# A decoder trunk whose instruction order comes from a planner: six of the planner's numbers and two orders changed

## Chip, cores, metric

One core of a Trainium2 chip runs the whole program. The metric is device time of one execution in microseconds (us). TensorE is called PE, VectorE DVE, ScalarE ACT, GpSimd POOL and SyncE, which issues the DMAs, SP, as in the profile.

## What is computed

Two layers over a sequence of 512 rows of 1024 numbers, all in float32. Of the reference, cut:

```python
for l in range(2):
    h = x @ w_in[l]                      # one projection for all branches
    a  = diff_attention(...)             # 4 heads, two maps each: p0 - lam * p1
    bo = dsa_attention(...)              # 4 query heads, one key/value head; an indexer of
                                         # 8 heads picks the 128 best keys of each query
    co = forgetting_attention(...)       # 4 heads, logits + cumulative log forget gate
    mixed = concat(a, bo, co) * silu(gate)
    x = layer_norm(alpha * x + mixed @ w_out[l])
```

## The kernel before

**Precision.** A float32 operand is split into a high part in fp32r and the rest (`split`: ACT casts the high part, then DVE or POOL subtracts it). A product takes three matmuls: high by high, low by high, high by low. Tiles ending in `h`/`hi` and `l`/`lo` are these parts (`xh`, `xl`, `whi`, `wlo`). All matmuls stand in `mm` (L375), all transpositions of 128 x 128 blocks in `transpose` (L378), all ACT work at L345, DVE work at L353, POOL work at L365, DMAs at L370.

**Units.** Attention goes by units of two heads or maps: `d` (differential), `f` (forgetting) and `s` (sparse), in the order of the table `UNITS` (L26). A unit runs over four blocks of 128 query rows (i = 0 to 3). For each block PE computes the scores of 128(i+1) keys into a PSUM bank `w`; DVE adds the mask and takes the minimum (`negm`, the form CUSTOM_DVE in the profile, ISA in an order); ACT takes the exponent (`p`); for `d` units DVE combines two maps, for `f` and `s` units ACT scales; PE transposes `p`; ACT and DVE split the result into `pt`; PE multiplies it with the values. There are eight PSUM banks for all of this and for the projections, so a matmul that opens a bank waits until the last reader of what stood there is done.

**Indexer and top-k.** `index_scores` (L887) fills the score tiles `acc` of blocks 1 to 3 from the four groups `iq`, of two indexer heads each, whose order stands in `HEAD` (L31). `topk` (L910) then takes, in 16 rounds per block, the 8 largest (MAX8) and strikes them out (MATCH_REPLACE8): 96 steps on DVE per layer, after which three TENSOR_SCALAR make masks of `acc`. The `s` units wait for these masks.

**Projections.** Between the units PE does the input projections of the layer, one block of 128 or 256 columns at a time. The weights of a block come as two halves (`raw`, 256 KB each, a ring of 4), and each half is split into `whi` and `wlo` (`Weights.prep`, L504). Query and key blocks go through the rotation: ACT copies the bank to `tg`, four DMAs swap the halves (`tg<-tg`), DVE and POOL multiply and add, ACT casts (`qk<-tg`), DVE or POOL subtract the rest, and for keys four DMAs copy between partition halves (`qk<-qk`).

**The order.** The kernel doesn't leave the order to a scheduler. `Flow` (L109) is a planner that runs while the program is built: `run` picks the first task, by priority, whose condition holds at the planned time of PE, and every instruction gets a planned start from a cost and from the latencies between engines. `emit` writes the instructions in the order of these starts. On the chip each engine then works through its own list in that order and waits on semaphores, whatever the plan thought of the time. SP's list is one queue too: a DMA that waits for its source holds up those behind it.

The numbers that the change touches are used in these places:

```python
flow.issue("pe", width(o) / 2.262 + 2, ...)                      # mm, L374
return min(self.gap(key, self.now, cond[2])[1] - SLACK, cond[3]) # ready_at, L267
yield "idle", "dve", cost + 100, start + TOPK_SPAN * n / 96      # topk, L919
... max(w.ready.values()) <= flow.now + READY for w in blocks)   # can_go, L1184
ready = split(hi[:, c], lo[:, c], raw, 0 if self.early else PREP_BIAS)  # prep, L515
```

The first is the planned time of a matmul on PE in ns. By the second and third a top-k step goes out when the plan sees a gap on DVE within `SLACK` ns, and at the latest at its share of `TOPK_SPAN`. By the fourth a projection may be chosen when its weights will be split within `READY` ns. In the last, `PREP_BIAS` is how many ns later than DVE the plan lets POOL end a subtraction for weights and still gives it to POOL; it counts while a top-k is under way.

Of the kernel before, what the change touches and what calls it, by code (L numbers as in the profile page):

```python
# [22 lines left out]
NEG = -1e30  # L23
TAKEN = -3e38
TOPK = min(256, S // 4)
UNITS = [("d", 0), ("f", 1), ("f", 0), ("d", 1), ("d", 3), ("d", 2), ("s", 1), ("s", 0)]  # L26
CONSTS = 3 * 512 + 128 + 9

LATE = 6
EARLY = 3  # L30
HEAD = [("kk", 0), ("dk", 0), ("dq", 0), ("dv", 0), ("iq", 1), ("iq", 0), ("iq", 3), ("iq", 2)]  # L31
INDEX_AT = 1
EXTRA = [("gate", 4)]
PROMPT = 5
# [4 lines left out]
BANKS = {"w": 8}  # L39
SHARE = {"proj": "w", "s": "w", "t": "w"}  # L40
RINGS = {"qk": 14, "tg": 7, "p": 4, "pt": 6, "vv": 4, "a": 2, "whi": 4, "wlo": 4}
SLACK = 1000
READY = 500
WAITING = 1
TOPK_SPAN = 112500
MARGIN = 0
BIAS = 2000
COLD = 5500
SPARE = 2
LNBIAS = 2000  # L50
LAST = 96
PREP_BIAS = 3500
RAW = 4

DQ, DK, DV = 0, 512, 1024
# [6 lines left out]
def early(l):  # L62
    return HEAD[:EARLY] + ([] if l else EXTRA)


def plan(l):
# [28 lines left out]

    for nm, j in early(l) + HEAD[EARLY:]:
        add(nm, j)
    for f, j in UNITS:
        for nm in {"d": ("dq", "dk", "dv"), "s": ("sq",), "f": ("fq", "fk", "fv")}[f]:
# [9 lines left out]
class Flow:  # L109
# [148 lines left out]
    def ready_at(self, cond):  # L258
# [7 lines left out]
        if kind == "idle":  # L266
            return min(self.gap(key, self.now, cond[2])[1] - SLACK, cond[3])  # L267
        times = sorted(self.banks[SHARE.get(key, key)] if kind == "bank" else self.free[key])
# [29 lines left out]
def tile_hybrid_decoder(  # L298
# [26 lines left out]
    flow = Flow()  # L325


    def width(ap):
        n = 1
        for d in ap.shape[1:]:  # L330
            n *= d
        return n
# [34 lines left out]
    def dma(o, i):  # L367
        inside = [v for v in (o, i) if not v.tensor.name.startswith(("in_", "out_"))]
        outs, ins = [v for v in inside if v is o], [v for v in inside if v is i]
        return flow.issue("sp", 640 if ins else 475, outs, ins, lambda: nc.sync.dma_start(o, i),  # L370
                          width(o) * o.shape[0] * 4)

    def mm(o, lhsT, rhs, **kw):
        flow.issue("pe", width(o) / 2.262 + 2, [o], [lhsT, rhs],  # L374
                   lambda: nc.tensor.matmul(o, lhsT, rhs, **kw))  # L375

    def transpose(o, i):
# [12 lines left out]
    def split(hi, lo, src, bias=BIAS):  # L390
        flow.set("high", act(hi, src))
        return either(lo, src, hi.bitcast(F32), OP.subtract, bias)
# [102 lines left out]
    class Weights:  # L495
# [8 lines left out]
        def prep(self):  # L504
# [6 lines left out]
            for k0 in range(0, len(self.ks), size):  # L511
                c = slice(k0, min(k0 + size, len(self.ks)))
                raw = tile_of([512], "raw", RAW)[:, :(c.stop - k0) * self.m].rearrange("p (k c) -> p k c", c=self.m)
                dma(raw, src[:, c])
                ready = split(hi[:, c], lo[:, c], raw, 0 if self.early else PREP_BIAS)  # L515
                self.high = flow.ev["high"] if k0 == 0 else self.high
# [32 lines left out]

    EORDER = [{"d": 0, "s": 4, "f": 6}[f] + j for f, j in UNITS]  # L550
    groups, number, order, first, nearly = [], {}, {}, [], []
# [229 lines left out]
    def causal(i):  # L781
        return cmask[:, 384 - 128 * i:512]
# [127 lines left out]
    def topk(l, acc):  # L910
        start, n = flow.now, 0
        flow.pressed = True
        for rnd in range(TOPK // 8):
            for i in (3, 2, 1):
                cost = 133 * (i + 1) + 69
                m8 = small([8], "m8", 6)
                for f in (lambda: vec("max", m8, acc[i], n=128 * (i + 1)),
                          lambda: vec("match_replace", acc[i], m8, acc[i], TAKEN)):
                    yield "idle", "dve", cost + 100, start + TOPK_SPAN * n / 96  # L919
                    f()  # L920
# [73 lines left out]
    def pair_unit(l, f, j):  # L994
        if f == "s":
# [3 lines left out]
            key = done[l, "kk", 0][0]  # L999
            keys, used = (key, key), q if (f, j) != UNITS[-1] else [*q, *key]  # L1000
            masks = [causal(0), acc[1], acc[2], acc[3]]
# [110 lines left out]
    def attention(l):  # L1112
        for at, (f, j) in enumerate(UNITS):
            if at == INDEX_AT:
# [4 lines left out]
    def projections(l):  # L1119
# [4 lines left out]
        else:  # L1124
            for nm, j in HEAD[:EARLY]:
                flow.add(PRIO_FILL, rope_group(l, nm, j))
# [43 lines left out]
    def later_projections(l):  # L1170
# [8 lines left out]
        def can_go(nm, j):  # L1179
# [3 lines left out]
            return sum(t <= flow.now for t in flow.free[tag]) >= n and \  # L1183
                all(w.ready and max(w.ready.values()) <= flow.now + READY for w in blocks)  # L1184
        while todo:
# [223 lines left out]
```

## Time and profile before

| | us |
|---|---|
| median of 3 executions (lowest, highest) | 610.49 (609.52, 612.15) |
| the profiled execution | 611.96 |
| its span, first to last instruction | 610.1 |
| PE busy in the span | 595.8 |
| DVE, ACT, POOL busy | 525.2, 403.0, 203.8 |

The page shows one execution. Its busy time of PE overlaps, since a matmul starts before the one ahead of it has ended: PE's pace is read from the distance of two starts, and a wait from the idle time before an instruction and from who ended it. The granted clock has two levels, 2.4 GHz (1.0) and 1.2 GHz (0.5).

### The profile page before, as it was taken

Reading aid. Unit: us, or ns where it says so; the run is one execution under the profiler, and the core shown is the slowest. Engines: PE = TensorE matmul, PEld = TensorE weight load, DVE = VectorE, ACT = ScalarE, POOL = GpSimd, SP = SyncE. Lnnn points to the kernel's source line nnn. Section 1 sums busy time; section 2 is a strip of 40 time slices with the busy share of each in tenths; the row PEclk is TensorE's granted clock in tenths of the full one; section 3 lists DMA queues with packets and bytes.
Section 4 is the critical chain, followed back from the end, with each engine's and each line's share of the span. In section 5 each row is a group of like instructions: output and inputs, shape, how many; then the busy total and the mean of one; then the engine's idle time right before and its main releaser. Section 6 shows DMA issues by size and latency. Waiting matters only on the chain.

```text
span 610.1 us, 10685 instructions
## 1 busy us (share of the span) xinstructions
PE 595.8 (98%) x3385; PEld 524.5 (86%) x3385; DVE 525.2 (86%) x1348; ACT 403.0 (66%) x1033; POOL 203.8 (33%) x209
## 2 busy tenths in 40 slices
PE   8999999999899999999999999999999999999994
PEld 7899998788888888888899999888898888888883
DVE  6599999999899997786867899999999999587766
ACT  6458775887568779962334778768957776887410
POOL 0015121357768910000001442042777794100000
PEclk9999999999899999999999999999999999999998
DMA  8565323324163422645235543134234343252402
GB/s 306 161 175 169 112 71 95 114 61 129 30 181 82 137 76 77 199 126 174 82 107 157 168 131 118 39 105 117 76 116 124 101 124 101 71 190 87 139 34 105
DMA packets 42681, 72.71 MB, mean 119 GB/s; under 512 B 6784, under 2 KB 10368, under 8 KB 42624
## 3 DMA queue, kind: packets, MB, share of 16 engines
q1 hardware_dynamic: 42624, 72.03, 38.9%
q8 instruction: 27, 0.44, 0.3%
q14 instruction: 30, 0.25, 0.1%
HBM read 53.13 MB, written 4.19 MB: 94 GB/s over the span
## 4 chain that ended last, share of the span: by engine, by line
PE 84%; DVE 8%; ACT 4%; issue 1%; POOL 1%; DMA 1%; SPq 0%; POOLq 0%; DVEq 0%; ACTq 0%
PE w L375 79%; PE w L378 5%; DVE acc L353 2%; ACT p L345 2%; DVE m L353 1%; DVE qk L353 1%; DVE p L353 1%; DMA raw<-in_w_packed_dram 1%; DVE tg L353 1%; DVE wlo L353 1%; DVE w L353 1%; ACT w L345 0%; ACT whi L345 0%; SPq L370 0%; ACT qk L345 0%
## 5 line engine op out<-in xcount | busy, mean ns | idle before, releaser
L375 PE MATMUL w<-xh,whi 128*128 128x512 f32 (+2 forms) x456 | 176.8, 389 | 0.0
L375 PE MATMUL w<-xh,wlo 128*128 128x512 f32 (+2 forms) x456 | 169.5, 373 | 0.0
L375 PE MATMUL w<-xl,whi 128*128 128x512 f32 (+2 forms) x456 | 169.4, 373 | 0.0
L345 ACT ACTIVATE whi<-raw 128x512 fp32r<-128x512 f32 (+1 forms) x156 | 90.3, 612 | 40.7 <-DMA raw<-in_w_packed_dram 33.1
L365 POOL TENSOR_TENSOR wlo<-raw,whi 128x512 fp32r<-128x512 f32 x57 | 72.9, 1297 | 112.0 <-ACT whi L345 91.2
L375 PEld LDWEIGHTS w<-xh,wlo 128*128 128x128 f32 x456 | 85.8, 188 | 14.3
L375 PEld LDWEIGHTS w<-xl,whi 128*128 128x128 f32 x456 | 86.6, 190 | 10.0
L375 PEld LDWEIGHTS w<-xh,whi 128*128 128x128 f32 x456 | 86.6, 190 | 10.0
L375 PE MATMUL w<-whi,xh 128*128 128x256 f32 (+2 forms) x240 | 76.3, 318 | 1.9 <-ACT p L345 1.9
L353 DVE TENSOR_TENSOR wlo<-raw,whi 128x512 fp32r<-128x512 f32 (+1 forms) x99 | 63.3, 675 | 14.7 <-ACT whi L345 14.2
L375 PE MATMUL w<-wlo,xh 128*128 128x256 f32 (+2 forms) x240 | 75.7, 315 | 0.0
L375 PE MATMUL w<-whi,xl 128*128 128x256 f32 (+2 forms) x240 | 75.5, 315 | 0.0
L375 PE MATMUL w<-qk 128*128 128x256 f32 (+3 forms) x352 | 71.8, 327 | 0.0
L375 PEld LDWEIGHTS w<-qk 128*128 128x128 f32 x352 | 56.7, 189 | 5.8
L345 ACT ACTIVATE p<-w,negm 128x128 f32<-128x128 f32 (+3 forms) x96 | 49.9, 523 | 14.9 <-DVE negm L353 14.2
L353 DVE MAX8 m<-acc 128x8 f32<-128x512 f32 (+2 forms) x96 | 52.6, 551 | 0.2
L365 POOL TENSOR_TENSOR tg<-tg,cst 128x512 f32<-128x512 f32 (+1 forms) x24 | 30.4, 1267 | 65.5 <-DMA tg<-tg 65.3
L353 DVE MATCH_REPLACE8 acc<-m,acc 128x512 f32<-128x512 f32 (+2 forms) x96 | 52.0, 542 | 0.0
L353 DVE CUSTOM_DVE_ANT_0 w<-w,cst 128x128 f32<-128x128 f32 (+3 forms) x104 | 47.6, 491 | 3.4 <-PE w L375 3.1
L375 PEld LDWEIGHTS w<-whi,xh 128*128 128x128 f32 x240 | 46.0, 191 | 4.3 <-ACT p L345 2.3
L375 PEld LDWEIGHTS w<-whi,xl 128*128 128x128 f32 x240 | 46.0, 192 | 2.2 <-DVE xl L353 0.2
L375 PEld LDWEIGHTS w<-wlo,xh 128*128 128x128 f32 x240 | 46.1, 192 | 1.8
(132 smaller groups left out, 1132.5 us busy)
## 6 DMA issues: line engine op xcount, KB each, us to landing
raw<-in_w_packed_dram SPq DMA_DIRECT2D x124, 256.0 KB, 3.2
raw<-in_w_out_dram SPq DMA_DIRECT2D x32, 256.0 KB, 2.9
qk<-qk SPq DMA_DIRECT2D x56, 128.0 KB, 2.3
tg<-tg SPq DMA_DIRECT2D x88, 64.0 KB, 2.0
raw<-in_w_packed_dram SPq DMA_DIRECT2D x16, 166.0 KB, 3.1
pt<-in_xT_dram SPq DMA_DIRECT2D x8, 256.0 KB, 5.6
tg<-tg SPq DMA_DIRECT2D x32, 48.0 KB, 1.9
vv<-in_ln_g_dram SPq DMA_DIRECT2D x2, 512.0 KB, 5.4
```

Of the source, the lines that this page charges most:

```text
L345: lambda: nc.scalar.activation(o, i, func, **kw))
L353: lambda: getattr(nc.vector, name)(o, *args, **kw), port=two_ports(name, o, ins))
L365: lambda: getattr(nc.gpsimd, name)(o, *args, **kw), port=name != "memset")
L375: lambda: nc.tensor.matmul(o, lhsT, rhs, **kw))
L378: flow.issue("pe", 109.0, [o], [i, ident], lambda: nc.tensor.transpose(o, i, ident))
```

## The change

The planner's numbers change: a matmul is planned with 4 ns instead of 2 on top of its width, and with 107 ns at least, so that one of 128 columns counts 107 ns instead of 59; `SLACK` is halved, `READY` is four times as long, `TOPK_SPAN` and `PREP_BIAS` grow. The two `s` units and the first two `iq` groups change places.

```diff
--- before.py
+++ after.py
@@ -23,12 +23,12 @@
 NEG = -1e30
 TAKEN = -3e38
 TOPK = min(256, S // 4)
-UNITS = [("d", 0), ("f", 1), ("f", 0), ("d", 1), ("d", 3), ("d", 2), ("s", 1), ("s", 0)]
+UNITS = [("d", 0), ("f", 1), ("f", 0), ("d", 1), ("d", 3), ("d", 2), ("s", 0), ("s", 1)]
 CONSTS = 3 * 512 + 128 + 9
 
 LATE = 6
 EARLY = 3
-HEAD = [("kk", 0), ("dk", 0), ("dq", 0), ("dv", 0), ("iq", 1), ("iq", 0), ("iq", 3), ("iq", 2)]
+HEAD = [("kk", 0), ("dk", 0), ("dq", 0), ("dv", 0), ("iq", 0), ("iq", 1), ("iq", 3), ("iq", 2)]
 INDEX_AT = 1
 EXTRA = [("gate", 4)]
 PROMPT = 5
@@ -39,17 +39,17 @@
 BANKS = {"w": 8}
 SHARE = {"proj": "w", "s": "w", "t": "w"}
 RINGS = {"qk": 14, "tg": 7, "p": 4, "pt": 6, "vv": 4, "a": 2, "whi": 4, "wlo": 4}
-SLACK = 1000
-READY = 500
+SLACK = 500
+READY = 2000
 WAITING = 1
-TOPK_SPAN = 112500
+TOPK_SPAN = 120000
 MARGIN = 0
 BIAS = 2000
 COLD = 5500
 SPARE = 2
 LNBIAS = 2000
 LAST = 96
-PREP_BIAS = 3500
+PREP_BIAS = 4000
 RAW = 4
 
 DQ, DK, DV = 0, 512, 1024
@@ -371,7 +371,7 @@
                           width(o) * o.shape[0] * 4)
 
     def mm(o, lhsT, rhs, **kw):
-        flow.issue("pe", width(o) / 2.262 + 2, [o], [lhsT, rhs],
+        flow.issue("pe", max(width(o) / 2.262 + 4, 107.0), [o], [lhsT, rhs],
                    lambda: nc.tensor.matmul(o, lhsT, rhs, **kw))
 
     def transpose(o, i):
```

What PE has to compute stays as it was. Thirteen subtractions, multiplications and additions go from DVE to POOL (DVE has 1241 rows of work instead of 1254, POOL 227 instead of 214, each instruction counted), among them three of `wlo`, six of `qk` and three of `tg`. The top-k of layer 0, from the first MAX to the three mask scalings, spreads over 301 DVE instructions instead of 293. The rest is order. Three places:

**PE, the first `f` unit after the indexer, layer 0.** Before: the last score matmul of the unit's block 1 (`w_338`), nine projection matmuls of 512 columns, and the transpositions of block 0 (`w_353`, `w_354`).

```order
L375 MATMUL w_338<-cc2_298,ccq1_75 128x256
L375 MATMUL w_323<-xh_72,whi_289 128x512
L375 MATMUL w_323<-xl_73,whi_289 128x512
L375 MATMUL w_323<-xh_72,wlo_290 128x512
L375 MATMUL w_323<-xh_72,whi_289 128x512
L375 MATMUL w_323<-xl_73,whi_289 128x512
L375 MATMUL w_323<-xh_72,wlo_290 128x512
L375 MATMUL w_323<-xh_72,whi_289 128x512
L375 MATMUL w_323<-xl_73,whi_289 128x512
L375 MATMUL w_323<-xh_72,wlo_290 128x512
L378 MATMUL w_353<-cst_66,p_330 128x128
L378 MATMUL w_354<-cst_66,p_332 128x128
```

The same place in the change; the scores of block 1 end with `w_319`, and 24 matmuls of 256 columns and 6 of 512 stand between them and the transpositions of block 0 (`w_335`, `w_336`), of which these are the last 8:

```order
L375 MATMUL w_304<-whi_257,xl_73 128x256
L375 MATMUL w_304<-wlo_258,xh_72 128x256
L375 MATMUL w_334<-xh_72,whi_270 128x512
L375 MATMUL w_334<-xl_73,whi_270 128x512
L375 MATMUL w_334<-xh_72,wlo_271 128x512
L375 MATMUL w_334<-xh_72,whi_270 128x512
L375 MATMUL w_334<-xl_73,whi_270 128x512
L375 MATMUL w_334<-xh_72,wlo_271 128x512
L378 MATMUL w_335<-cst_66,p_311 128x128
L378 MATMUL w_336<-cst_66,p_313 128x128
```

Nine matmuls of 512 columns ahead of the transpositions have become six of 512 and 24 of 256.

**SP, the weight halves that come in while a key block is copied, layer 0 (about 144 to 151 us in the trace of before).** Before: two halves, the copies of the key block `qk_460` to `qk_463` in between the four of `tg_472`, and then the next two halves.

```order
L370 DMA raw_469<-in_w_packed_dram 128x512
L370 DMA raw_470<-in_w_packed_dram 128x512
L370 DMA tg_472<-tg_471 32x512
L370 DMA qk_460<-qk_460 64x512
L370 DMA qk_462<-qk_462 64x512
L370 DMA qk_461<-qk_461 64x512
L370 DMA qk_463<-qk_463 64x512
L370 DMA tg_472<-tg_471 32x512 x3
L370 DMA raw_481<-in_w_packed_dram 128x512
L370 DMA raw_482<-in_w_packed_dram 128x512
```

The same place in the change:

```order
L370 DMA raw_466<-in_w_packed_dram 128x512
L370 DMA raw_467<-in_w_packed_dram 128x512
L370 DMA tg_469<-tg_468 32x512 x4
L370 DMA raw_485<-in_w_packed_dram 128x512
L370 DMA qk_472<-qk_472 64x512
L370 DMA qk_474<-qk_474 64x512
L370 DMA qk_473<-qk_473 64x512
L370 DMA raw_486<-in_w_packed_dram 128x512
L370 DMA qk_475<-qk_475 64x512
```

The four `tg` copies stand together, the first of the next two halves (`raw_485`) has moved ahead of the key copies, and the second (`raw_486`) stands behind three of them.

**ACT, the first scores of the last `d` unit, layer 0 (about 200 to 205 us in the trace of before).** Before, the two casts of a weight half pair, two of a query block, and the exponents of block 0 of the unit:

```order
L345 ACTIVATE tg_648<-w_630 128x512
L345 ACTIVATE rr_650<-tot_554 128x4
L345 ACTIVATE whi_644<-raw_646 128x512
L345 ACTIVATE whi_644<-raw_647 128x512
L345 ACTIVATE qk_639<-tg_628 64x512
L345 ACTIVATE qk_640<-tg_628 64x512
L345 ACTIVATE p_657,tot_652<-w_655,negm_656 128x128
L345 ACTIVATE w_654,tot_652<-w_654,negm_658 128x128
```

The same place in the change:

```order
L345 ACTIVATE tg_647<-w_635 128x512
L345 ACTIVATE rr_649<-tot_551 128x4
L345 ACTIVATE whi_643<-raw_645 128x512
L345 ACTIVATE whi_643<-raw_646 128x512
L345 ACTIVATE p_657,tot_652<-w_655,negm_656 128x128
L345 ACTIVATE w_654,tot_652<-w_654,negm_658 128x128
L345 ACTIVATE qk_640<-tg_633 64x512
L345 ACTIVATE qk_641<-tg_633 64x512
```

The two casts of the query block have moved behind the exponents; the two weight casts still stand ahead of them. Behind these rows PE transposes this `p` 3.6 us of matmuls after the scores, where it was 4.7 (counted in PE's list at 0.23 us for 512 columns, 0.12 for 256 and 0.11 for 128).

## Rows read from the trace of the kernel before

**Rows 1.** The page, sections 1 and 2: busy time by engine; granted TensorE clock.
```profile
PE 595.8 (98%) x3385; PEld 524.5 (86%) x3385; DVE 525.2 (86%) x1348; ACT 403.0 (66%) x1033; POOL 203.8 (33%) x209
...
PEclk9999999999899999999999999999999999999998
```

**Rows 2.** The page, section 4: the chain that ended last, by engine.
```profile
PE 84%; DVE 8%; ACT 4%; issue 1%; POOL 1%; DMA 1%; SPq 0%; POOLq 0%; DVEq 0%; ACTq 0%
```

**Rows 3.** Stretches: length; busy us PE, PEld, DVE, ACT, POOL; PEclk, DMA share, GB/s.
```profile
100.00:125.00 25.00, 24.00 (x126) 19.56 (x125) 23.88 (x71) 17.26 (x44) 7.64 (x6) 1.00 0.38 105
140.00:160.00 20.00, 18.10 (x120) 16.30 (x118) 18.35 (x55) 12.38 (x29) 15.00 (x12) 1.00 0.34 93
160.00:180.00 20.00, 20.00 (x123) 18.35 (x124) 18.50 (x64) 13.66 (x43) 12.47 (x10) 0.91 0.42 120
390.00:410.00 20.00, 19.74 (x96) 16.15 (x95) 19.07 (x50) 12.57 (x31) 5.70 (x5) 1.00 0.36 105
440.00:460.00 20.00, 20.00 (x151) 19.05 (x149) 19.18 (x60) 11.70 (x31) 15.16 (x13) 1.00 0.38 106
601.00:610.10 9.10, 0.25 (x3) 0.05 (x1) 5.18 (x14) 0.47 (x1) 0.54 (x1) 0.72 0.27 102
```

**Rows 4.** Timeline of PE, 109 to 113 us: start, duration, instruction, [idle before <-releaser].
```profile
109.72 0.39 PE L375 MATMUL w<-xl,whi 128*128 128x512 f32 x1
109.94 0.39 PE L375 MATMUL w<-xh,wlo 128*128 128x512 f32 x1
111.07 0.62 PE L378 MATMUL w<-cst,p 128*128 128x128 f32 x2 [0.74 <-ACT p L345]
```

**Rows 5.** Timeline of PE, 157 to 163 us.
```profile
159.94 0.38 PE L375 MATMUL w<-whi,xh 128*128 128x256 f32 x1 [1.90 <-ACT p L345]
...
160.28 0.28 PE L375 MATMUL w<-wlo,xh 128*128 128x256 f32 x1
160.40 0.28 PE L375 MATMUL w<-whi,xh 128*128 128x256 f32 x1
...
162.29 0.41 PE L375 MATMUL w<-whi,xl 128*128 128x256 f32 x1
162.51 0.41 PE L375 MATMUL w<-wlo,xh 128*128 128x256 f32 x1
```

**Rows 6.** Timeline of SP (DMA issue), 143 to 154 us.
```profile
144.27 3.21 SPq L370 DMA_DIRECT2D qk<-qk  x4
...
149.43 1.08 SPq L370 DMA_DIRECT2D raw<-in_w_packed_dram  x2
```

**Rows 7.** Timeline of ACT, 152 to 160 us.
```profile
154.40 0.63 ACT L345 ACTIVATE whi<-raw 128x512 fp32r<-128x512 f32 x1 [0.29 <-DMA raw<-in_w_packed_dram]
...
158.02 1.28 ACT L345 ACTIVATE qk<-tg 64x512 fp32r<-64x512 f32 x2 [2.64 <-POOL tg L365]
```

**Rows 8.** Timeline of POOL, 154 to 158 us.
```profile
156.69 1.30 POOL L365 TENSOR_TENSOR tg<-tg 128x512 f32<-128x512 f32 x1
```

**Rows 9.** Timeline of ACT in layer 1, 447 to 450 us.
```profile
448.33 1.34 ACT L345 ACTIVATE whi<-raw 128x512 fp32r<-128x512 f32 x2 [0.17 <-DMA raw<-in_w_packed_dram]
```

**Rows 10.** Timeline of ACT, 203 to 206 us.
```profile
203.59 1.29 ACT L345 ACTIVATE qk<-tg 64x512 fp32r<-64x512 f32 x2 [0.58 <-POOL tg L365]
204.90 0.37 ACT L345 ACTIVATE p<-w,negm 128x128 f32<-128x128 f32 x1
```

**Rows 11.** Groups of DVE by form: busy us, mean ns of one.
```profile
L353 DVE TENSOR_TENSOR qk<-tg,qk 64x512 fp32r<-64x512 f32 x14 | 11.2, 797 | 0.5 <-ACT qk L345 0.2
L353 DVE TENSOR_TENSOR qk<-w,qk 64x512 fp32r<-64x512 f32 x16 | 11.0, 685 | 0.5 <-ACT qk L345 0.3
```

**Rows 12.** Busy time over the top-k of layer 0 (columns as in group 3).
```profile
100.30:217.10 116.80, 113.90 (x646) 98.59 (x645) 110.77 (x343) 84.36 (x230) 76.29 (x62) 0.99 0.38 108
```

**Rows 13.** Timeline of DVE, 216 to 224 us.
```profile
216.22 0.89 DVE L353 TENSOR_SCALAR acc<-acc 128x512 f32<-128x512 f32 x3
...
223.34 0.46 DVE L353 CUSTOM_DVE_ANT_0 w<-w,acc 128x256 f32<-128x256 f32 x1
```

## Prediction

> **What bounds the kernel now.** I read the page's busy times first: PE is busy 595.8 of a span of 610.1 us, and no other engine comes near it [rows 1]. That sum counts overlapping matmuls more than once, so it hides some idle time, but the chain of waits says the same: 84% of it runs over PE [rows 2]. A change of order therefore pays only where PE stood idle or ran at the lower clock. Next I looked for such places, with busy times by stretch, where a PE sum below the stretch's length is idle time that can't be hidden. After 601 us PE works 0.25 of 9.10 us [rows 3]: the last matmul is over, and DVE, ACT and POOL finish the layer norm. That tail of about 8.9 us has the same instructions in the change. Of the 14.3 us that PE's busy time lacks, some 5.4 remain. Three places have names: 100 to 125 lacks 1.00, 140 to 160 lacks 1.90 and 390 to 410 lacks 0.26 [rows 3]. The other 2.2 us are the start and small change. The granted clock then shows one more loss: 0.91 of full speed in 160 to 180 although PE is busy all through [rows 3]. The reader is to see there that an idle time is paid twice, as the stop and as the slow matmuls after it.
>
> **The pair place, layer 0 (−1.0).** PE's timeline shows 512-column matmuls that start 0.22 apart, and at 111.07 a transposition that had waited 0.74 us for an exponent `p` of ACT [rows 4]; with smaller waits around it the stretch lacks 1.00. `p` was late against PE's list, not against a fixed time: between scores and transpositions stood nine matmuls of 512, 9 x 0.23 = 2.1 us. Now it is 6 x 0.23 + 24 x 0.12 = 4.3 us (0.12 is the distance of two 256-column matmuls in [rows 5]). The added 2.2 us of cover are more than twice the missing 1.0, so I take all of it, −1.0; bounds 0 (ACT as much later as PE) and −1.0. The same place in layer 1 is the 0.26 of 390 to 410: −0.26, bounds 0 and −0.26.
>
> **The late weight half, layer 0 (−3.7).** At 159.94 PE waited 1.90 us for an exponent that had to free its bank [rows 5]. I followed it back. ACT could not take that exponent before two `qk` casts, which it began at 158.02 after waiting 2.64 us for POOL's `tg` [rows 7]. POOL did that `tg` at 156.69, 1.30 us long [rows 8], behind subtractions of weights, which follow ACT's `whi` cast; and that cast, at 154.40, had waited for a DMA [rows 7]. The DMA was issued only at 149.43, since four copies of the key block held SP's queue for 3.21 us from 144.27 on, with three `tg` copies after them [rows 6]. After the stop PE starts its 256-column matmuls 0.22 apart instead of 0.12 [rows 5]: half clock, 1.2 GHz. What that cost is in the stretch: (1 − 0.91) x 20 = 1.8 us. Together 1.90 + 1.8 = 3.7 us.
> In the change the four `tg` copies stand together, the first of the two halves is ahead of the key copies and the second behind three of them. The first no longer pays the 3.21 us of the key copies, the second about a quarter less, and both no longer stand behind the split `tg` copies: between 2.4 and 5.1 us earlier, from the issue times of [rows 6]. The wait to be removed is 1.90. Against it goes little: PE's list asks for the bank at another point, by some 1 us either way, as the order of PE and ACT stands. The trace has a control: in layer 1 of before, where the `tg` copies aren't split, ACT's `whi` cast waits 0.17 instead of 2.64 behind it [rows 9], and PE has no idle time in 440 to 460 [rows 3]. So −3.7; bounds 0 (the stop only moves) and −3.7. Next late would be the second half.
>
> **The new place, last `d` unit (+0.4).** The two `qk` casts, 1.29 us [rows 10], moved behind the exponents, so `p` can start 1.29 earlier than behind them at 204.90; but the transposition follows the scores after 3.6 us of PE's work instead of 4.7, 1.1 less. On balance nothing is late. If the weight casts ahead of the exponents wait for their DMA, though, the cover is 1.1 thinner. Bounds 0 and +1.2 in each layer; I take 0.2 each, near the balance: +0.4.
>
> **Thirteen subtractions and sums from DVE to POOL (0).** DVE is relieved of 13 x 0.7 to 0.8 us, 9 to 10 us [rows 11]; POOL, busy 203.8 us [rows 1], takes 13 x 1.30 = 17 us [rows 8]. Both lie beside PE's work, and POOL has room: 76.29 of 116.80 in the tightest stretch [rows 12]. What POOL's work does to DVE shows in one pair of forms: with both inputs in SBUF the subtraction takes 797 ns, with one in PSUM 685 [rows 11], so at most 13 x 0.11 = 1.4 us come back on DVE, hidden too.
> The Trainium skill, "SBUF — State Buffer", section "SBUF: two separate sides", speaks against this part of the change: a GpSimd instruction that reads SBUF and a VectorE instruction with two SBUF inputs share one port pair, held for the whole instruction, and the loser blocks fully. By that rule the 13 x 1.30 = 17 us could all come back as DVE waits, a net +7 us on DVE instead of −9. The difference of 112 ns in [rows 11] is far from a full block, so this trace doesn't bear out the full price.
>
> **Top-k spread.** It runs 116.80 us, with DVE busy 110.77 [rows 12], 95%, PE 113.90. Over 301 instead of 293 DVE instructions, and about ten us more of PE's work, DVE's share falls to an estimated 90%, which gives the softmax steps between room. What the longer top-k uses up is slack at its end: the mask scaling runs at 216.22, the first masked reduction at 223.34 [rows 13], with some 6 us between; counted in the order about 4 us of that go, 2 remain. Cost 0; if this cover goes too, each us late is a us of PE in each layer. The swapped `s` units and `iq` groups issue the same instructions: 0. `SLACK`, `READY` and the longer planned matmuls act only by the order, which is counted above.
>
> **Sum.** −1.0 − 0.26 − 3.7 + 0.4 = −4.6 us. Durations are from the profiled execution, 611.96, which lies 1.5 above the median of 610.49; against its own time the sum gives 607.4, against the median 605.9. I forecast **605.9**.
>
> **Rivals.** 0.5% of 610.49 is about what a measurement of this kernel can tell from no change: 3.05 us, so faster is below 607.4 and slower above 613.5.
> - *More goes*: the remaining 2.2 us of small idle times shrink as well, since exponents get ahead of casts everywhere. 605.9 − 2.2, and about 0.4 for the new place: 603.3. For it: DVE has room. Against: the small ones are spread over the whole span.
> - *Re-dealt*: the gaps close and as many open elsewhere, since a new order of 3385 matmuls makes new tight places. One stop with half clock (3.7) and one pair place (1.0) back: 605.9 + 4.7 = 610.6, no change. For it: an idle time of only 1.9 us here cost 3.7, and every unit has such places. Against: before has only one large one in 600 us.
> - *The blocked DVE*: POOL's 17 us stop DVE inside the top-k, where 116.80 − 110.77 = 6.0 us are free [rows 12]; the 7 us net split over two layers are 3.5 each, more than the 2 of slack at the end: 2 x 1.5 = +3 on 605.9, 609. This is the price that the Trainium skill's rule on that page would have; the 797 and 685 ns speak against it.
> - *Slower: late half blocks hold ACT*. At the last `d` unit two weight casts stand ahead of the exponents, in both layers, and at the late-half place the second half stands behind three key copies. If a half lands later than its cast is due, ACT, which takes its list in order, holds the exponents and PE stops, at the price of the old gap: 3.7. Two places in two layers: 14.8 − 1.3 − 3.7 = +9.8, 620.3; the last `d` unit alone in both layers: 7.4 − 5.0 = +2.4, 612.9. It decides if the halves land more than about 1.5 us later than worked out. For it: such a wait is what made the old gap [rows 7]. Against: elsewhere the casts wait 0.17 to 0.29 [rows 7, 9].
> - *The change doesn't do what it says* is not open: the rows of the order have moved.
>
> **How the numbers follow.** Forecast 0.52, its own range 604 to 609, of which 0.38 lie below 607.4 and 0.14 above; more goes 0.10, faster; re-dealt 0.20 and blocked DVE 0.05, no change; slower 0.13. So faster 0.48, same 0.39, slower 0.13. The range 603 to 612 takes in the forecast's bounds, most of the first rival, and the re-dealt case with its spread of 1.5; it leaves out the slower one and a few hundredths on either side.
>
> **What would show it.** Right: no transposition waiting 0.7 us near 111; no 1.9 us stop near 158 to 160; PEclk at 1.0 in that stretch; the `whi` casts there not waiting, nor ACT 2.64 us for `tg`. Wrong: PE idle for more than 1 us at the first scores of the last `d` unit (about 200 and 495) behind a `whi` cast that waits for its DMA; masked reductions that wait for the mask scalings; two-input DVE forms well above 797 ns. A new PE stop of 2 us with half clock anywhere makes the forecast wrong by the whole of its largest term.

## Result: slower by 0.56%, and where the time went

Each kernel was timed in 16 executions: 614.18 us median (612.98 to 616.64) for the change, 610.83 (609.46 to 612.73) for the kernel before; the ratio is 1.0056, 95% interval 1.0045 to 1.0068. The forecast was 605.9 us, the range 603 to 612. The profiled execution of the change took 613.87 us.

The page of the changed kernel answers to [rows 1, 2] with these lines (busy time by engine, granted clock, chain by engine):

```profile
PE 599.1 (98%) x3384; PEld 522.9 (85%) x3384; DVE 518.1 (85%) x1335; ACT 401.0 (66%) x1033; POOL 218.1 (36%) x222
...
PEclk9999999999999999999999999999999999999998
...
PE 58%; DVE 18%; ACT 9%; DMA 6%; POOL 4%; issue 3%; SPq 2%; POOLq 0%; DVEq 0%; ACTq 0%
```

DVE is busy 7 us less, POOL 14 us more; the prediction counted 9 to 10 and 17. But the chain that ended last runs over PE for 58% instead of 84%, and over DVE for 18% instead of 8%: in this chain PE now stands behind other engines at many places. Busy time by stretch of the changed kernel, columns as in [rows 3]:

```profile
40.00:102.00 62.00, 61.14 (x374) 55.30 (x373) 57.55 (x133) 44.09 (x115) 20.13 (x33) 1.00 0.43 124
100.00:125.00 25.00, 25.00 (x138) 21.10 (x138) 23.72 (x74) 19.39 (x50) 10.15 (x8) 1.00 0.23 63
140.00:160.00 20.00, 20.00 (x141) 18.53 (x140) 17.59 (x45) 13.37 (x31) 14.65 (x13) 1.00 0.46 119
160.00:180.00 20.00, 19.82 (x120) 17.31 (x119) 19.35 (x70) 14.24 (x46) 13.23 (x11) 1.00 0.49 138
363.00:403.00 40.00, 39.84 (x237) 34.37 (x236) 37.41 (x82) 28.41 (x71) 7.96 (x9) 1.00 0.24 74
463.00:504.00 41.00, 40.38 (x214) 33.57 (x213) 38.71 (x126) 30.00 (x93) 30.75 (x27) 1.00 0.43 125
```

The kernel before in the three of these stretches that are not among [rows 3]:

```profile
40.00:102.00 62.00, 62.00 (x381) 57.62 (x380) 59.05 (x132) 46.31 (x119) 17.40 (x31) 1.00 0.39 119
363.00:403.00 40.00, 40.00 (x239) 35.91 (x237) 37.62 (x71) 28.06 (x63) 6.58 (x6) 1.00 0.31 95
463.00:504.00 41.00, 41.00 (x222) 34.96 (x221) 39.89 (x126) 30.95 (x95) 33.61 (x29) 1.00 0.44 125
```

The named places are full now: 25.00 where 24.00 stood, 20.00 where 18.10 stood, the clock at 1.00 where it was 0.91. New idle time shows where there was none. It looks small, since a matmul's recorded duration (0.34 us for 384 columns) is longer than the distance to the next (0.17): a delay shorter than the overlap leaves no idle time. PE's waits over the whole span show how much stays hidden (operation waited for: us in total, times, longest; the 1.5 for `junk` is the start). Of the kernel before:

```profile
PE w L375 <- ACT p L345: 1.9, 1, 1.9
PE w L375 <- DVE junk L353: 1.5, 1, 1.5
PE w L378 <- ACT p L345: 1.3, 3, 0.7
PE w L378 <- DVE p L353: 0.7, 2, 0.4
```

Of the change:

```profile
PE w L375 <- DVE junk L353: 1.5, 1, 1.5
PE w L378 <- DVE p L353: 0.9, 3, 0.4
PE w L375 <- DVE qk L353: 0.4, 2, 0.3
PE w L375 <- DVE a L353: 0.4, 2, 0.2
PE w L375 <- DVE pt L353: 0.2, 1, 0.2
PE w L375 <- DMA qk<-qk: 0.2, 1, 0.2
```

By this view the change waits less (2.1 against 3.9 us). So I counted PE's loss from the distances of starts: the time of a stretch less its matmuls at their undisturbed distances (0.228 us for 512 columns, 0.174 for 384, 0.152 for 332, 0.119 for 256, 0.110 for 128). The stretches hold the same amount of PE work in each kernel:

| from (us, in the trace of before) | loss before | loss after |
|---|---|---|
| 43, indexer and first units, layer 0 | 0.80 | 3.85 |
| 103, both named stops of layer 0 | 5.98 | 1.10 |
| 185, last `d` unit, layer 0 | 0.28 | 1.23 |
| 225, end of layer 0, start of layer 1 | 2.35 | 2.70 |
| 366, indexer, layer 1 | 0.11 | 1.81 |
| 405, the pair place, layer 1 | 0.89 | -0.03 |
| 426 | 0.09 | 0.89 |
| 464 to 505, last `d` units, layer 1 | 0.17 | 2.00 |
| from the first projection to the last matmul | 13.48 | 15.68 |

The stops gave back 4.88 + 0.92 = 5.8 us, a little more than forecast. In the other six stretches of the table 8.7 us came in; what lies ahead of 43 us and behind 505 lost 0.7 us less. Giving each delay of over 0.06 us to what ended PE's last wait ahead of it, ACT held PE for 4.6 us before and 0.9 after, DVE for 1.6 before and 6.7 after.

The table sets one execution of each kernel beside one of the other. That of before lies 1.1 us above its median and that of the change 0.3 below, so the table shows 2.2 of the 3.35 us by which the medians differ. How far one execution can stray, the profile of the run only_units (below) shows: up to 230 us its lists are those of before, and yet its first stretch lost 3.7 us instead of 0.80. PE waited 1.24 us for DVE's `qk` at 44.68, and the granted clock fell:

```profile
40.00:60.00 20.00, 18.48 (x102) 17.71 (x101) 18.51 (x56) 13.56 (x44) 9.06 (x23) 0.91 0.57 171
```

In four other profiles with these lists (before_cover, before_sp, before_best, before_best2) the first stretch lost 0.2 to 1.6 us, while the change lost 3.85 there, and 3.91 in a second profile with its lists (after_notopk). So the loss recurs in the change, but a single row of the table can be off by 3 us in one execution.

### The profile page after: what moved, and what is told of

Its sections match the earlier page's. It is cut to its first block, busy times and chain, and to the rows that moved or that the text cites. A ratio compares the mean times of both kernels' runs of the same rounds, so it can differ in the third digit from the quotient of the medians.

```text
span 612.1 us, 10710 instructions
## 1 busy us (share of the span) xinstructions
PE 599.1 (98%) x3384; PEld 522.9 (85%) x3384; DVE 518.1 (85%) x1335; ACT 401.0 (66%) x1033; POOL 218.1 (36%) x222
## 4 chain that ended last, share of the span: by engine, by line
PE 58%; DVE 18%; ACT 9%; DMA 6%; POOL 4%; issue 3%; SPq 2%; POOLq 0%; DVEq 0%; ACTq 0%
PE w L375 54%; DMA raw<-in_w_packed_dram 5%; PE w L378 4%; DVE acc L353 3%; DVE tg L353 2%; ACT whi L345 2%; ACT p L345 2%; DVE p L353 2%; DVE m L353 2%; SPq L370 2%; DVE wlo L353 2%; POOL tg L365 1%; DVE w L353 1%; DVE qk L353 1%; ACT w L345 1%
## 5 line engine op out<-in xcount | busy, mean ns | idle before, releaser
L365 POOL TENSOR_TENSOR wlo<-raw,whi 128x512 fp32r<-128x512 f32 x60 | 76.5, 1295 | 102.4 <-ACT whi L345 90.5
L365 POOL TENSOR_TENSOR tg<-tg,cst 128x512 f32<-128x512 f32 (+1 forms) x27 | 34.8, 1288 | 77.1 <-DMA tg<-tg 77.0
L365 POOL TENSOR_TENSOR qk<-tg,qk 64x512 fp32r<-64x512 f32 (+1 forms) x36 | 45.8, 1271 | 15.5 <-ACT qk L345 14.1
L345 ACT ACTIVATE qk<-tg 64x512 fp32r<-64x512 f32 (+1 forms) x60 | 36.0, 600 | 21.0 <-POOL tg L365 13.9
L365 POOL TENSOR_TENSOR rs<-rs,half 128x1 f32<-128x1 f32 x8 | 4.8, 596 | 124.3 <-DVE rs L353 124.3
```

The source lines that it names most:

```text
L345: lambda: nc.scalar.activation(o, i, func, **kw))
L365: lambda: getattr(nc.gpsimd, name)(o, *args, **kw), port=name != "memset")
```

## Experiments

In all of them the kernel before was timed on the same chip; "over before" is the difference of the two medians. The change itself is +3.35 us.

### One number at a time

The three edits that alter PE's list from its early part on, each alone in the kernel before, and the first of them taken out of the change:

```diff
# only_mm
-        flow.issue("pe", width(o) / 2.262 + 2, [o], [lhsT, rhs],
+        flow.issue("pe", max(width(o) / 2.262 + 4, 107.0), [o], [lhsT, rhs],
# only_head
-HEAD = [("kk", 0), ("dk", 0), ("dq", 0), ("dv", 0), ("iq", 1), ("iq", 0), ("iq", 3), ("iq", 2)]
+HEAD = [("kk", 0), ("dk", 0), ("dq", 0), ("dv", 0), ("iq", 0), ("iq", 1), ("iq", 3), ("iq", 2)]
# only_span
-TOPK_SPAN = 112500
+TOPK_SPAN = 120000
# but_mm: the change, with
-        flow.issue("pe", max(width(o) / 2.262 + 4, 107.0), [o], [lhsT, rhs],
+        flow.issue("pe", width(o) / 2.262 + 2, [o], [lhsT, rhs],
```

only_mm:

> The kernel before with the new planned time of a matmul alone (4 ns on top, 107 ns at least); everything else as before. Theory M (margin): the old planned time of a short matmul, 59 ns where the trace shows 110, made the plan believe that PE comes early, so the plan put other work in and PE in fact found its operands ready; with the true time PE is packed tight and small waits appear. M expects most of the loss here: 612.5 to 615.5 us against about 610.8. Theory H (the swapped iq groups) and theory S (the longer top-k) expect 609.5 to 611.5. Theory R (re-dealt: any new order loses or wins some us by chance) expects no fixed sign, up to 5 us either way.

but_mm:

> The changed kernel with the old planned time of a matmul put back. M expects the loss to go: 609 to 611.5 us, with small waits of PE in the first 100 us back near the 0.8 us of before. H and S expect it to stay: 613 to 615. R: no fixed value, the effect need not be the opposite of the one of that part alone.

only_head:

> The kernel before with the first two iq groups swapped, nothing else. H expects the loss here, since the new small waits begin at 43 us, in the scores of the indexer: 612.5 to 615. M and S expect 610 to 611.5. R: anything within 5 us.

only_span:

> The kernel before with the longer TOPK_SPAN alone. S expects the loss here, the top-k of layer 0 ending later: 612.5 to 615. M and H expect 609 to 611.5, M a little under before because DVE is less dense in the top-k. R: anything within 5 us.

Measured: only_mm 625.37 (ratio 1.024, 1.0222 to 1.0259), but_mm 622.71 (1.0205, 1.0182 to 1.0229), only_head 625.79 (1.0248, 1.0229 to 1.0266), only_span 629.72 (1.0315, 1.0299 to 1.0331). Nothing had expected 12 to 20 us. The effects don't add: three edits of +15, +16 and +20 us are part of a change of +3, and taking one out of it makes it worse by 9. In the three single edits most of it is lost at the end of layer 0 (the row "225" of the table, where they lose 11 to 12 us more than before); but_mm loses 3 us more there and 6 in the first stretch. The stretches at the layer's end of only_head (columns as in [rows 3]):

```profile
252.00:262.00 10.00, 4.95 (x31) 4.11 (x29) 9.65 (x24) 9.26 (x26) 0.73 (x1) 0.96 0.29 101
262.00:272.00 10.00, 8.55 (x27) 6.48 (x28) 6.39 (x14) 7.16 (x16) 0.73 (x1) 0.52 0.00 0
```

Of only_span:

```profile
252.00:262.00 10.00, 6.77 (x36) 4.95 (x34) 6.97 (x19) 8.75 (x21) 0.00 (x0) 0.89 0.20 67
262.00:272.00 10.00, 6.23 (x23) 4.76 (x24) 8.20 (x12) 5.05 (x11) 2.11 (x2) 0.60 0.14 50
```

Of the kernel before, full and at full clock:

```profile
252.00:262.00 10.00, 10.00 (x59) 8.53 (x58) 9.01 (x16) 9.77 (x20) 1.24 (x1) 1.00 0.23 77
262.00:272.00 10.00, 10.00 (x46) 8.19 (x45) 8.89 (x15) 5.12 (x10) 1.24 (x1) 1.00 0.52 149
```

PE's timeline of only_head shows why: after the last scores of the last `s` unit no projection is left to fill the softmax, and PE waits for each step, then works at half clock.

```profile
255.15 1.18 PE L375 MATMUL w<-qk 128*128 128x512 f32 x4
256.17 0.40 PE L375 MATMUL w<-pt,vd 128*128 128x256 f32 x2
259.34 0.39 PE L375 MATMUL w<-pt,vd 128*128 128x256 f32 x1 [2.77 <-ACT pt L345]
262.01 1.01 PE L375 MATMUL w<-pt,vd 128*128 128x256 f32 x3 [2.29 <-DVE pt L353]
```

In the kernel before and in the change 24 and 39 projection matmuls stand there, counted in PE's lists, in only_head none. So the time of an order is decided in good part by the projections that the planner still has at the layer's end, which no local reading of a changed place shows. Their number alone doesn't give the price: only_span has 9 left and only_mm 18, none of them behind the last transpositions, and both lose about as much as only_head. Theory R of the expectations (an order is re-dealt as a whole) fits in kind, not in size, since it allowed 5 us either way; M, H and S, which look for one guilty number, all fall.

The fourth edit that moves rows, the swapped units, alone:

```diff
# only_units
-UNITS = [("d", 0), ("f", 1), ("f", 0), ("d", 1), ("d", 3), ("d", 2), ("s", 1), ("s", 0)]
+UNITS = [("d", 0), ("f", 1), ("f", 0), ("d", 1), ("d", 3), ("d", 2), ("s", 0), ("s", 1)]
```

> The kernel before with the two s units swapped, nothing else. PE's list then differs in 143 rows, all near the layers' ends; the same work stands there. 610 to 611.5, no difference in either theory.

611.29 us, ratio 1.000 (0.9981 to 1.0019): nothing, as forecast. `READY` and `PREP_BIAS` alone leave every list of the kernel before as it is, `SLACK` alone moves a few rows on DVE; they were not run.

### Is it cover that PE lacks?

Counted in PE's lists at the distances above, the median work between the scores of an `f` or `s` block and its transposition is 6.9 us before, 5.8 after, 6.0 with the new matmul time alone, 6.4 in the change without it. That speaks for a lack of cover. The test moves PE rows alone: the numbers are places in an engine's list, and the group goes ahead of the first one (cut).

```diff
-        for _, _, f in sorted(self.order, key=lambda o: o[:2]):
-            f()
+        for o in moved(sorted(self.order, key=lambda o: o[:2])):
+            o[2]()
...
+MOVES = [(211, [223, 224, 225]), (213, [226, 227, 228]), (233, [234, 235, 236]), (252, [254, 255, 256]),
...
+    for at, group in MOVES:
+        for m in group:
+            order.remove(pe[m])
+            order.insert(order.index(pe[at]), pe[m])
```

> The changed kernel with PE's list edited by hand in 16 places where its trace shows PE waiting 0.15 to 0.58 us, mostly for DVE: three projection matmuls that stood behind the waiting matmul (and whose operands were long there) are put ahead of it. The lists of DVE, ACT, POOL and SP stay the same row for row. Theory C (cover: the plan left too little PE work between a block's steps, DVE itself is in time) expects the waits at these places to go: 608.5 to 611 us against 614.2 of the changed kernel. Theory D (DVE is full in these stretches and sets the pace, so that a wait only moves to the next step) expects less than 1.5 us: 612.7 to 614.5.

614.04 us, +2.7 over before, ratio 1.0058 (1.0037 to 1.0079) where the change stood at 1.0056: no gain worth the name. The first stretch lost 5.57 us instead of 3.85: the waits moved to the next step of each block. Theory C falls. The same at three places of the kernel before (306, 343 and 408 us):

> The kernel before with the same kind of edit at the three places that its trace offers (306, 343 and 408 us, 0.60, 0.44 and 0.42 us of wait): C expects 609 to 610 against 610.5; D no change. The two large stops at 111 and 160 us can't be filled this way, since the next projections there wait for the same banks: they stay in both theories.

610.41, ratio 0.9992 (0.9972 to 1.0012), -0.9 over before: about the gain that C expects, not clear of zero.

### Less work on DVE

Two experiments take work off DVE and leave every other list as it is. The first leaves the top-k's steps out:

```diff
-        lambda: getattr(nc.vector, name)(o, *args, **kw), port=two_ports(name, o, ins))
+        lambda: name in ("max", "match_replace") or getattr(nc.vector, name)(o, *args, **kw), port=two_ports(name, o, ins))
```

> The changed kernel without the 192 steps of the top-k on DVE (MAX8 and MATCH_REPLACE8 left out, the masks are made from the raw scores); everything else in the same order on every engine. If the DVE waits of 102 to 222 and 395 to 512 us are due to the top-k that fills DVE (D), PE's losses there fall from about 5 to 2 us and the time to 609.5 to 612; those of 41 to 102 and 363 to 395 us stay, since no top-k runs there. If only the lack of cover in PE's list counts (C), DVE in time or not, less than 1 us goes in the stretches with the top-k: 613 to 614.5.

> The kernel before without the same 192 steps. Its two large stops, at 111 and 160 us, were read as ACT's and a DMA's, not DVE's: if so they stay, and the time is 608.5 to 610.5. If DVE was behind them after all, 605 to 608.

The change falls to 610.83 us (-0.5 over before, so 3.9 less than the change), the kernel before to 609.22 (-2.1). Both lose the same 192 steps, and the difference between the two kernels shrinks from 3.35 to 1.6 us. In the change the loss of 464 to 505 goes from 2.00 to 0.70 and that of 185 to 225 from 1.23 to 0.33, while that of the first stretch, where no top-k runs, stays (3.91): as D has it; the end of layer 0 lost some 0.9 us more. In the kernel before, the large stop stays, but the pair place is full, which I had not expected:

```profile
100.00:125.00 25.00, 25.00 (x136) 21.03 (x135) 14.23 (x44) 19.38 (x51) 7.18 (x7) 1.00 0.37 106
140.00:160.00 20.00, 17.32 (x118) 15.99 (x117) 9.00 (x28) 10.59 (x26) 13.71 (x12) 0.97 0.30 80
```

The second experiment is for the stretches without a top-k. It replaces subtractions of `wlo` by memsets:

```diff
-        lambda: getattr(nc.vector, name)(o, *args, **kw), port=two_ports(name, o, ins))
+        lambda: nc.vector.memset(o.bitcast(F32), 0.0) if LIGHT else getattr(nc.vector, name)(o, *args, **kw), port=two_ports(name, o, ins))
```

> The changed kernel with 26 subtractions of wlo on DVE, all those of 37 to 103 and 361 to 388 us, replaced by memsets to zero of the same tiles (the low parts of these weight halves are left out of the products); all five lists keep their order. A memset is planned at 335 ns against 601. Theory D: DVE's amount of work sets PE's pace there, about 7 us are taken off it, and the losses of 41 to 102 and 363 to 403 us (3.6 and 2.2 us) fall to under 1.5 and 1.2: 610.5 to 612.5 us. Theory K: a chain over PE, DVE and ACT sets the pace: 613.3 to 614.5.

> The same in the kernel before, 30 subtractions of the same stretches. PE loses under 1 us there, so both theories expect no more than 0.8 us: 610 to 611.2.

The change goes to 611.60 us (ratio to before 1.0008, 0.9991 to 1.0025; the change stood at 1.0056), 2.4 us less; the first stretch loses 1.90 instead of 3.85, the one at 366 1.46 instead of 1.81. The kernel before gains 0.6 (0.9981, 0.9962 to 1.0001), so the difference between the two kernels is 1.5 us here. The time is what theory D expected, but the losses did not fall to its 1.5 and 1.2. A memset took 485 ns where the subtraction took 684, so some 5 us were taken off DVE and not 7. It also reads nothing and so doesn't wait for ACT's `whi` cast, for which DVE sat idle 1.7 us in 37 to 103 of the change: a part of the gain may be theory K's. Theory D holds as far as this: what PE waits for in the change is, for about half of the difference in each experiment, the time that DVE needs for its list; the two were not run together. It is not that DVE has more to do there: it is busy 57.55 us of 62 in the change and 59.05 before. It gets to the steps that PE wants later against PE's list.

### Moving DVE's work instead of removing it

If DVE's work holds PE, it could go to POOL, or behind the wanted steps. Both were tried, with every PE, ACT and SP row in place.

```diff
# after_dp: 13 subtractions of wlo, at their place of the order
-        lambda: getattr(nc.vector, name)(o, *args, **kw), port=two_ports(name, o, ins))
+        lambda: getattr(nc.gpsimd if SWAP else nc.vector, name)(o, *args, **kw), port=two_ports(name, o, ins))
# after_order: on DVE's list, (place, goes behind place)
+LATER = [(80, 83), (81, 83), (87, 94), (105, 111), (109, 111), (117, 123), (118, 123),
+         (142, 148), (143, 148), (322, 325), (662, 668), (663, 668), (687, 692), (688, 692), (853, 855), (867, 870)]
# after_both: LATER and the MOVES of after_cover
```

after_dp:

> The changed kernel with 13 subtractions of wlo in the first stretches of both layers (37 to 103 and 361 to 387 us) put from DVE to POOL at the same place of the order; their results are wanted 2 to 24 us later. PE's, ACT's and SP's lists stay the same. Theory D (in these stretches DVE sets PE's pace): the loss of 41 to 102 and 363 to 403 us, 5.8 us, falls by 2 to 4 us, time 610.5 to 612.5. Theory K (a chain PE, DVE, ACT, DVE, PE sets the pace, not the amount of DVE's work): less than 1 us, 613 to 614.5; more than that if POOL's own chain of small steps is held up.

616.59 us, +5.6 over before: worse than the change by 2.2. DVE's timeline of after_dp at the first place:

```profile
38.17 2.12 DVE L353 TENSOR_TENSOR qk<-tg,qk 64x512 fp32r<-64x512 f32 x2 [1.52 <-ACT qk L345]
```

POOL's, at the same time:

```profile
36.47 2.56 POOL L353 TENSOR_TENSOR wlo<-raw,whi 128x512 fp32r<-128x512 f32 x2 [3.21 <-ACT whi L345]
```

DVE's timeline of the change, at that place and at another:

```profile
39.01 1.39 DVE L353 TENSOR_TENSOR qk<-tg,qk 64x512 fp32r<-64x512 f32 x2
...
63.02 1.40 DVE L353 TENSOR_TENSOR wlo<-raw,whi 128x512 fp32r<-128x512 f32 x1
64.34 0.54 DVE L353 TENSOR_TENSOR tg<-w,cst 128x384 f32<-128x384 f32 x1
64.81 0.68 DVE L353 TENSOR_TENSOR pt<-w,pt 128x512 fp32r<-128x512 f32 x1
```

Two subtractions that take 1.39 us together take 2.12 when they begin while POOL subtracts: the first ends only after POOL's second has, at 36.47 + 2.56 = 39.03. In the change itself one such subtraction took 1.40 instead of 0.69 us, at 63.02, under a POOL multiplication of 62.59 to 63.87, and PE then waited for the `pt` behind it (0.48 us late at 65.54). Over the forms of two inputs in SBUF such delays sum to 4.9 us before, 4.8 in the change and 12.0 in after_dp, in 9, 10 and 19 instructions, every one of which began while POOL was at work: of the 9 us taken off DVE 7 came back. The experiment therefore doesn't tell D from K; it shows why work can't simply go to POOL.

after_order and after_both:

> The changed kernel with DVE's list edited by hand at 10 places: 12 subtractions of wlo, three MATCH_REPLACE8 of the top-k and one more of them, which stood ahead of a step that PE was waiting for and whose own results are wanted 4 to 20 us later, go behind that step. The lists of PE, ACT, POOL and SP stay the same row for row, DVE does the same work. Theory O (order within DVE's list) expects the waits at these places, about 2.9 us, to go: 610.5 to 612.5 us against 614.2. Theory D (amount) and K (chain): no more than 1 us, 613 to 614.5, since the same work is done one after the other.

> The same with the 16 PE edits of after_cover on top. O and C together (cover helps once the wanted steps come first): 608.5 to 611. O alone: as after_order within 0.7 us. D and K: 613 to 614.5.

620.08 (+9.0) and 619.44 us (+8.4): all theories miss. The first stretch lost 8.65 us. The work that went behind a wanted step came to stand ahead of the next wanted ones (at 76 us PE waited 1.6 us for DVE's `acc`, and the clock of 80 to 102 was 0.94; that of 363 to 403 was 0.96). How long its own result can wait says nothing about who stands behind it on DVE. Theory O falls in this form; that a better placing exists is not excluded.

### The two stops of before, and a kernel faster than both

The largest term of the prediction was a chain from SP's list to PE. The test moves two DMAs of the kernel before up SP's list, ahead of a copy that waits for its source:

```diff
+EDITS = [("sp", 118, [126, 127])]
```

> The kernel before with SP's list edited by hand at one place of layer 0: the two weight halves that its trace shows issued at 149.43 us go ahead of the tg copy of 143.64, in the 5 us in which SP waits for that copy's source. All other engines' lists stay the same row for row. The prediction's term for this stop was 3.7 us, 1.90 of idle time and 1.8 of half clock after it. If the chain was read rightly the stop near 158 to 160 us goes: 607 to 609 us against 610.5 to 611 (3.7 if every execution pays the half clock, about 2 if only some do). If the stop has another cause: 610 to 611.5.

609.13 us, ratio 0.9972 (0.9956 to 0.9988), -1.9 over before. The chain was read rightly; PE's idle time there falls from 1.90 to 0.56 us (before_sp, with the pair place above it):

```profile
100.00:125.00 25.00, 24.21 (x127) 19.71 (x126) 23.90 (x74) 17.48 (x47) 7.18 (x6) 1.00 0.35 101
140.00:160.00 20.00, 19.44 (x134) 17.77 (x133) 19.27 (x57) 12.79 (x31) 16.23 (x14) 1.00 0.33 81
```

But the term is 1.9, not 3.7. The half clock after the stop is not in every execution: the profile of before_cover, with that place of the lists untouched, has the stop without it.

```profile
140.00:160.00 20.00, 18.46 (x122) 16.65 (x122) 18.62 (x56) 12.81 (x31) 15.33 (x13) 1.00 0.33 90
160.00:180.00 20.00, 20.00 (x130) 18.12 (x130) 19.44 (x66) 14.37 (x47) 13.02 (x11) 1.00 0.48 143
```

How often it comes, the timed executions of the kernel before tell: of the 99 with a clock on record 41 have a mean granted clock of 0.993 or less, with a median of 612.03 us, and 58 one of 0.994 or more, with a median of 610.26. The two groups lie 1.8 us apart, as much as was read off the profile. In before_sp 2 of 12 executions have the lower clock. So the 1.9 reads as 1.3 us of idle time and a spell of half clock that goes from a part of the executions. Where the spell lies in executions without a profile is not on record; in only_units it followed another stop.

The next version adds, at the pair place of both layers, DVE's four mask-and-minimum steps ahead of the MAX8 and MATCH_REPLACE8 before them, and the PE edits of before_cover; the last one puts that MATCH_REPLACE8 behind the reciprocal too:

```diff
# before_best
+EDITS = [("sp", 118, [126, 127]), ("dve", 183, [185, 186, 187, 188]), ("dve", 735, [737, 738, 739, 740]),
+         ("pe", 1657, [1661, 1662, 1663]), ("pe", 1931, [1932, 1933, 1934]), ("pe", 2319, [2329, 2330, 2331])]
# before_best2, besides
+LATER = [("dve", 184, 189), ("dve", 736, 741)]
```

> The kernel before with that SP edit, the three PE edits of before_cover, and in each layer the four mask-and-minimum steps of the first f unit after the indexer ahead of the MAX8 and MATCH_REPLACE8 that stand before them on DVE (about 108 and 404 us; the stop at 111 went from a loss of 2.1 to 0.5 us without the top-k, so those two steps hold it up). Expected if the terms add: about 2 to 3.7 for SP, 1.0 to 1.5 for DVE, 1.2 for PE: 604.5 to 607. If the stops are re-dealt, 608 to 611.

> before_best with the MATCH_REPLACE8 that now stands ahead of the reciprocal of the first f unit put behind it, in both layers (there p waited 0.78 us for that reciprocal, and PE 0.69 at 109 us). O expects 0.5 to 1 us less than before_best: 607 to 607.7. Otherwise 608 to 608.5.

608.07 (0.9954, 0.9936 to 0.9972) and 607.85 us (0.995, 0.9935 to 0.9964): both faster than the kernel before by about 3 us and so than the change by about 6, under the gain expected (604.5 to 607). The last edit gives 0.2, less than a measurement tells. The pair place of layer 0 was not filled: 24.22 us with DVE's edit below, 24.21 without it in before_sp, and 24.27 in before_best2. The exponents started earlier, but `p` then waited for the reciprocal behind the two top-k steps, and PE 0.53 us for `p`; in before_best2 it waited 0.26. So of the 3 us the SP edit alone gave 1.9, and the rest can't be shared out between DVE's and PE's edits. Of before_best:

```profile
100.00:125.00 25.00, 24.22 (x127) 19.69 (x126) 23.93 (x74) 17.56 (x47) 7.08 (x6) 1.00 0.36 100
140.00:160.00 20.00, 19.43 (x134) 17.75 (x133) 19.26 (x57) 12.80 (x31) 16.19 (x14) 1.00 0.32 80
160.00:180.00 20.00, 20.00 (x125) 17.79 (x125) 19.48 (x66) 13.87 (x45) 13.10 (x11) 1.00 0.50 146
```

## Why the prediction was wrong

- **What bounds the kernel:** right for before; but "a change of order therefore pays only where PE stood idle" is half of it. It can cost wherever PE did not stand idle.
- **The pair place (-1.0 and -0.26):** the effect came: 25.00 of 25 us, and the losses of both layers went. The cause was read one engine short: ACT's `p` was late because of the top-k on DVE, as before_notopk shows, where the place is full. The two steps ahead of DVE's minimum are not enough to explain it, since the place stays open in before_best, where they stand behind it and ahead of the reciprocal.
- **The late weight half (-3.7):** the right chain, mis-sized. It measured 1.9: 1.3 of the stop, and the half clock in the share of executions that had it. The full 1.8 of half clock was in the profiled execution, 1.1 us above the median of 610.83, and I took it off the median as well.
- **The new place (+0.4):** it lost 0.95 us more in layer 0 (185 to 225) and 1.83 in layer 1 (464 to 505), mostly to DVE under the top-k, as after_notopk shows, and not to late weight casts; the bounds of 0 and +1.2 each were about right for the first and short for the second.
- **Thirteen operations to POOL (0):** DVE's busy time fell by 7.1 us, and the delays under POOL stayed at 4.9 and 4.8 us; the planner books the port of DVE and POOL like an engine (`port` in `slot`), and after_dp went around that. But the 112 ns per instruction by which I weighed the rule is a mean over 14, of which two were held for 0.6 and 1.0 us and twelve not at all [rows 11]. The Trainium skill, "SBUF — State Buffer", section "SBUF: two separate sides", says that the loser of the shared port blocks for the whole instruction; at 38.17 us of after_dp the trace agrees: the first subtraction ended 0.55 us after POOL's, and the pair took 0.73 us longer. Weighing it against a mean was the error, though not one that decided the time.
- **Top-k spread (0):** the end came as counted: 1.9 us between the mask scaling and the first masked reduction (217.44 + 1.41 to 220.77), with no wait of PE in the view. The room between did not: DVE is busy 113.67 of 120.56 us there, 94% instead of the 90% estimated, and with the top-k left out most of the losses of 185 to 225 and 464 to 505 go.
- **The step that failed:** "`SLACK`, `READY` and the longer planned matmuls act only by the order, which is counted above". It was counted at three places, and the rest stood in the sum at 0, while PE's list of some 2,700 rows (repeats as one, buffer numbers left out) differs in some 1,400, taken out and put in counted. Outside the named stops the change lost 8.7 us more in the profiled executions, 2.8 of it at the new place, for which 0.4 stood in the sum, and 5.9 where the sum had nothing. The rival *re-dealt* was of the right kind, but held 4.7 us and 0.20; *late half blocks*, the one that ended slower, did not come: no 2 us stop at the last `d` unit.
- **What the runs settle, and what not:** DVE's list holds PE in the change: less work on it takes away about half of the difference between the kernels, under the top-k (after_notopk) and outside it (after_light). A lack of PE work that a local edit could fill does not (after_cover). That the steps are packed closer (6.9 to 5.8 us) is counted in the lists, and the new matmul time is not alone in it (6.4 without it). That this is what makes DVE late is argued, not shown, since no run changed it without re-dealing the rest.

## What to carry to other kernels

Where a planner writes the order, a change of one of its numbers is a new order, not a local edit: price each place where PE had just enough cover, the end of each layer first, and don't sum the gains of the gaps that close. To keep the gain of a gap that has been understood, edit the list at that gap: a few such edits gave 3 us where six new planner numbers and two new orders lost 3. An edit that misreads the gap gives nothing, as at the pair place. And take a stop's price from several executions before it is set against a median.

## What the runs showed of the hardware

- A stop of PE of 1.5 to 1.9 us was followed by half clock in one execution and not in another: 0.91 in the stretch behind it in the kernel before, 1.00 in before_cover and in before_light (18.13 of 20 us busy in the stretch of the stop). Of 99 executions of the kernel before 41 had a mean clock of 0.993 or less, and were 1.8 us longer in the median.
- A DVE instruction with two inputs in SBUF that began while POOL worked was held for up to 0.99 us in before (9 of 28 such beginnings). What tells them apart is in the trace: all 9 began under a POOL instruction of 256 columns or more with at least 0.3 us left, and ended 0.55 us after it. Of the 19 that were not held 18 began under one of 1 to 16 columns, even with 0.98 us of it left, and one in the last 0.15 us of a wide one.
- A delay of PE shorter than the overlap of two matmuls (about 0.17 us at 384 columns) leaves no idle time and no wait in the profile; together they made up most of the 8.7 us, against 2.1 us of waits in the view.
